# Second score product of the 64-wide heads over 128 partitions instead of 64, with 33 instead of 30 big tiles

## Chip, cores and metric

The kernel runs on one core of a Trainium2 chip. The metric is the device time of one execution in microseconds. The kernel before took 2614.11 us (median of three runs, 2605.13 to 2625.22).

## What is computed

A two-layer encoder trunk over 1024 tokens of width 1024, in float32. Each layer is a mixer of two kinds of attention side by side, then a SwiGLU with 2816 hidden features, each with a scaled residual and a layer norm.

```python
for layer in range(DEPTH):
    if layer % 2 == 0:
        mix = _mixer_ab(x, ...)     # latent attention (8 heads) | sliding-window attention (8 heads, 2 k/v heads)
    else:
        mix = _mixer_cd(x, ...)     # forgetting attention (8 heads) | chunked attention with relative bias (8 heads)
    x = _layer_norm(DEEPNORM_ALPHA * x + mix, ln1_g[layer], ln1_b[layer])
    ffn = _swiglu(x, w_gate, w_up, w_down)
    x = _layer_norm(DEEPNORM_ALPHA * x + ffn, ln2_g[layer], ln2_b[layer])
```

Three of the four kinds have heads of 64 features whose scores are `q . k / 8` plus a bias: the sliding window (`swa`), the forgetting heads (`fox`) and the chunked heads. The latent heads have 96 features and are not touched by the change.

## The kernel before

**Products in two parts.** Float32 numbers are held as a high part of type float32r and the rest, a low part. A product of two such numbers is three matmuls into one PSUM tile (`mm3`, L127): high by high, high by low, low by high. A 64-wide head needs only half of the 128 rows of TensorE for one product, so two of the three are put into one matmul: for the fox and chunked heads, k lies as [high; low] over the 128 partitions and q as [high; high], and L591 in `qk64` contracts over all 128. The third product, q's low part by k's high part, contracts over 64 partitions (L592: rows `r : r + 64` of the tile `ql`, which two heads share, one in the upper and one in the lower half). The sliding-window heads do the same with the sides exchanged: q is [high; low], k is [high; high] (`kk`), L860 contracts over 128, and L861 multiplies q's high part by k's low part (`kl`, two k/v heads in one tile) over 64.

**Attention rows.** `attention_row` is one block of 128 queries of one head; `swa_row` is one block of four heads. A row has stages: `a` (scores on TensorE; L524 on VectorE adds the bias and takes the running maximum; L529 on ScalarE is the exponential), `n` (L533 reciprocal on VectorE, L534 the division on GpSimd), `t` (L551 transposes on TensorE, L106/L107 split into parts), `v` (L562 product with v), `m` (merge and store). A row of over 512 keys has its scores in two pieces, so two PSUM tiles. There are 16 rows of `swa` and, in layer 1, 16 heads of eight rows each. `stream` runs them as a software pipeline: at each step a new row does `a`, the row before it `n`, the one before that `t`, and so on, and between the stages `pump` lets in dense work that the next group needs (projections, L127 into tiles `pd`). The fox heads' bias tile comes from ScalarE or, for the block on the diagonal, from GpSimd (L718, L719).

**Projections of a pair of heads.** `pair_jobs` projects q and k for two heads; `q_evac` writes q's parts from PSUM: L606 high part on ScalarE, L607 a DMA that copies it into the other half, L608 low part on VectorE. GpSimd also makes the low parts of the weights (L117).

**Tiles and order.** The pool `gp` has 30 tiles of 128 x 1024 (`g`) which hold activations, q, k, v, x in both parts, and more. A tile's place is taken when a program instruction first writes it and is given back after its last reader; the Tile scheduler sets the order of each engine's instructions when the program is built, with the pools' free places as one of its conditions. All DMAs are issued from the queue of SyncE.

Of the kernel before, what the change touches and what calls it, by code (L numbers as in the profile page):

```python
# [14 lines left out]
ALU = mybir.AluOpType  # L15
# [5 lines left out]
P = 128  # L21
# [11 lines left out]
CFG = dict(gp=30, wrp=3, whp=5, sp=3, hp=3, bp=2, tp=2, pd=3, ps=2, pt=2, pv=1)  # L33


def fv(ap):
    return ap.bitcast(F32)


class Core:  # L40
# [137 lines left out]
    def ln_pipe(self, y, g, b, xt, done):  # L178
        """Layer norm of one token tile after the other, each one's stages apart; the last ones take the shortest way."""
# [30 lines left out]
    @staticmethod  # L210
    def feat(xt, k, half):
        """Features of tile k for half of the tokens, as a high and a low part."""
        return tuple(x[k // 2][half][:, k % 2, :] for x in xt)
# [6 lines left out]
    def winograd(self, r, b):  # L220
        """The four sums of 2 x 2 blocks that the one side of a product takes; b(i) is a block of the side, r their tiles."""
        for i, (x, z, op) in enumerate(b):
            self.nc.gpsimd.tensor_tensor(r[i], fv(x), fv(r[z] if isinstance(z, int) else z), op=op)

    def sums_x(self, xt):
        """Sums of blocks (feature tiles 0, 1, 4 or 2, 3, 5) x (half of the tokens), as lists of low and high parts by tile."""
# [32 lines left out]
    def cross(self, out, w, x, first, last):  # L259
        """High times low and low times high parts of a block."""  # L260
        for i, (a, b) in enumerate(zip(w, x)):
            self.nc.tensor.matmul(out, a, b, start=first and i == 0, stop=last and i == len(w) - 1)  # L262

    def gate_up(self, wg, wu, xt, xs, more):
        """Gate and up products of one tile for all tokens; over the first feature tiles, the products of high with low
        parts are a Winograd form of the 2 x 2 blocks (gate, up) x (features) x (tokens), with seven instead of eight."""
# [113 lines left out]
def chain(jobs):  # L380
    """Dense jobs (prep, body): each one's weights are fetched while the one before runs."""
    ready = jobs[0][0]()
    for i, (_, body) in enumerate(jobs):
        now, ready = ready, jobs[i + 1][0]() if i + 1 < len(jobs) else None
        yield from body(now)
# [7 lines left out]
class Mixers(Core):  # L393
    def stream(self, groups):
        """Rows of attention in a software pipeline; between their stages, the dense work that the next group needs."""
# [67 lines left out]
    def out_weights(self, wo, kts, j0, j1, tile):  # L463
        """Weights j0 to j1 of the eight that four row tiles of the output projection have."""
# [121 lines left out]
    def qk64(self, qt, ql, kt, r):  # L586
        nc = self.nc

        def f(p, i, c, w):
            q = slice(i * P, i * P + P)  # L590
            nc.tensor.matmul(p, qt[:, q], kt[:, c : c + w], start=True, stop=False)  # L591
            nc.tensor.matmul(p, ql[r : r + HD, q], kt[r : r + HD, c : c + w], start=False, stop=True)  # L592
# [3 lines left out]
    def pair_jobs(self, xt, wqk, i0, out, open_ln=None):  # L596
        """q and k of two 64-wide heads; k is [hi; lo] over the partitions, q is [hi; hi] and its low part apart."""
# [3 lines left out]
        def q_evac(p, o):  # L601
            if "q" not in tiles:
                tiles["q"] = out["q"] = [self.g() for _ in range(3)]
            qa, qb, ql = tiles["q"]
            for t, r in ((qa, 0), (qb, HD)):
# [50 lines left out]
    def mixer_cd(self, xt, wqk, wv, wf, bf, relb, o_scr, c_scr, out_early, open_ln):  # L656
# [18 lines left out]
        def make(n):  # L675
            def rows():
                typ, pair = n // 4, n % 4
                r = []
                for hh in range(2):
# [21 lines left out]
                    r += self.attention_rows(pre, self.qk64(qk[n]["q"][hh], qk[n]["q"][2], qk[n]["k"][hh], hh * HD),  # L701
# [23 lines left out]
    def forget_gate(self, xt, w, bf, c_scr):  # L725
# [17 lines left out]
        # min(z, 0) - log1p(exp(-|z|)), log1p(u) = 2 artanh(u / (2 + u))  # L743
# [33 lines left out]
    def swa_kv(self, xt, wqs, sinks, w):  # L777
# [5 lines left out]
        kk, kl = [self.g() for _ in range(2)], self.g()  # L783
        for half in range(2):
            o = slice(half * 512, half * 512 + 512)
            p = self.fproj(w, xt, half)
            for v in range(2):
# [3 lines left out]
                nc.vector.tensor_tensor(kl[r, o], p[r], fv(kk[v][r, o]), op=ALU.subtract)  # L791
# [50 lines left out]
    def swa_row(self, g, i, qs, bt, pre, o_scr):  # L842
        nc = self.nc
        kk, kl, vs, sk, nsk = self.swa_state
        zr = slice(g * HD, g * HD + HD)
# [7 lines left out]
        def a():  # L853
            sb = st["s"] = self.s().rearrange("p (h k) -> p h k", k=256)
            mx = self.m(4, "mx")
            for hp in range(2):
                p = self.pss().rearrange("p (h k) -> p h k", k=256)
                for z in range(2):
                    h = hp * 2 + z
                    nc.tensor.matmul(p[:, z, 0:kw], qs[h][:, q], kk[g][:, ks], start=True, stop=False)  # L860
                    nc.tensor.matmul(p[:, z, 0:kw], qs[h][zr, q], kl[zr, ks], start=False, stop=True)  # L861
# [375 lines left out]
```

## Time and profile before

| what | value |
|---|---|
| runs, median (lowest to highest) | 2614.11 us (2605.13 to 2625.22) |
| profiled execution, span | 2610.2 us |
| PE busy (matmul) | 2543.0 us, 97% |
| DVE, ACT, POOL busy | 52%, 37%, 52% |
| DMA, mean | 66 GB/s |

The span is read against its own engines: PE is TensorE's matmul row, PEld its weight loads, DVE is VectorE, ACT ScalarE, POOL GpSimd. A matmul's busy time has a modelled end, so it overlaps the next one's; what a matmul costs the queue is the distance to the next. The program runs the sliding window with the projections of the latent heads first (to some 205 us), then the latent heads, the output projection and the SwiGLU of layer 0 (to some 1180 us), then the fox and chunked heads of layer 1 (some 1235 to 1840 us), and then its output projection and SwiGLU.

### The profile page before, as it was taken

How to read it: one execution, taken by the hardware profiler on the slowest of the kernel's cores; microseconds unless marked ns; L12 is line 12 of the kernel's file. 1: busy time of each engine (PE TensorE's matmuls, PEld its weight loads, DVE VectorE, ACT ScalarE, POOL GpSimd, SP SyncE). 2: the span in 40 equal slices, each digit the busy share in tenths (PEclk: the TensorE clock that was granted, in tenths of full speed). 3: DMA queues.
4: the chain of work that ended last, by engine and by line, in shares of the span. 5: the costliest groups of instructions: out<-in, count | busy, mean ns of one | idle time of the engine just before them, and what ended most of it. 6: DMA issues, size and time to landing. Idle time of an engine off the chain costs nothing.

```text
span 2610.2 us, 35589 instructions
## 1 busy us (share of the span) xinstructions
PE 2543.0 (97%) x12376; PEld 2082.6 (80%) x12376; DVE 1360.7 (52%) x3096; ACT 970.9 (37%) x2112; POOL 1350.2 (52%) x1586
## 2 busy tenths in 40 slices
PE   8998999999999999999999999999899999999997
PEld 7976878788888888877778787877778888888886
DVE  3467766734444444447355555456734444444457
ACT  5366766422222222223355655454432222222221
POOL 3332465785555555555345443353765555555565
PEclk9999999999999999999999999999999999999999
DMA  4225241211111111122221111140211111111112
GB/s 149 71 79 166 73 133 53 67 45 53 49 49 49 49 54 56 53 70 97 68 62 50 55 43 50 41 160 26 85 37 49 54 52 49 49 53 49 49 53 97
DMA packets 103923, 172.66 MB, mean 66 GB/s; under 512 B 12728, under 2 KB 38712, under 8 KB 103744
## 3 DMA queue, kind: packets, MB, share of 16 engines
q1 hardware_dynamic: 103744, 170.39, 21.8%
q8 instruction: 98, 1.61, 0.3%
q14 instruction: 81, 0.66, 0.1%
HBM read 143.57 MB, written 22.58 MB: 64 GB/s over the span
## 4 chain that ended last, share of the span: by engine, by line
PE 87%; DVE 4%; POOL 3%; DMA 2%; ACT 2%; issue 1%; SPq 0%; POOLq 0%; DVEq 0%; ACTq 0%
PE pd L127 24%; PE ps L127 18%; PE pd L285 17%; PE pd L262 6%; PE pt L262 6%; PE pv L562 4%; PE pt L551 3%; PE ps L592 2%; PE pv L262 2%; PE ps L591 1%; POOL g L164 1%; DVE g L192 1%; DMA wr<-o_scr 1%; PE ps L861 1%; DVE m L162 1%
## 5 line engine op out<-in xcount | busy, mean ns | idle before, releaser
L117 POOL TENSOR_TENSOR wh<-wr,wh 128x512 fp32r<-128x512 f32 (+2 forms) x363 | 481.8, 1336 | 648.7 <-ACT wh L116 636.3
L127 PE MATMUL pd<-g,wh 128*128 128x512 f32 (+1 forms) x2076 | 540.1, 405 | 19.1 <-ACT g L106 10.1
L285 PE MATMUL pd<-g,wh 128*128 128x512 f32 x1984 | 501.7, 389 | 0.0
L116 ACT CAST wh<-wr 128x512 fp32r<-128x512 f32 (+2 forms) x363 | 222.1, 613 | 745.3 <-PE pd L285 429.1
L127 PEld LDWEIGHTS pd<-g,wh 128*128 128x128 f32 (+1 forms) x2076 | 381.1, 190 | 113.9 <-issue 15.0
L127 PE MATMUL ps<-wh,h 128*128 128x512 f32 x1920 | 462.1, 391 | 1.0 <-DVE g L365 1.0
L285 PEld LDWEIGHTS pd<-g,wh 128*128 128x128 f32 x1984 | 372.4, 188 | 77.3
L127 PEld LDWEIGHTS ps<-wh,h 128*128 128x128 f32 x1920 | 360.6, 188 | 77.7 <-DVE g L365 3.3
L365 DVE TENSOR_TENSOR g<-ps,g 128x512 f32<-128x512 f32 x288 | 197.1, 689 | 321.8 <-PE ps L127 321.8
L534 POOL TENSOR_SCALAR s<-s,m 128x128 f32<-128x128 f32 (+1 forms) x192 | 138.7, 723 | 203.1 <-DVE m L533 183.0
L107 DVE TENSOR_TENSOR h<-pt,h 128x512 fp32r<-128x512 f32 (+3 forms) x318 | 170.3, 544 | 74.1 <-ACT h L106 72.7
L106 ACT CAST h<-pt 128x512 fp32r<-128x512 f32 (+3 forms) x318 | 145.7, 473 | 149.4 <-PE pt L551 138.1
L562 PE MATMUL pv<-h,g 128*128 128x256 f32 x928 | 163.2, 297 | 4.0 <-ACT h L106 2.5
L529 ACT ACTIVATE s<-s,m 128x128 f32<-128x128 f32 (+1 forms) x192 | 144.0, 750 | 58.8 <-DVE m L527 51.6
L127 PE MATMUL pd<-wh,g 128*128 128x256 f32 (+2 forms) x1056 | 159.4, 297 | 0.0
L127 PEld LDWEIGHTS pd<-wh,g 128*128 128x128 f32 x1056 | 141.5, 192 | 7.1 <-issue 5.0
L296 DVE TENSOR_TENSOR t<-pd,t 128x512 f32<-128x512 f32 x160 | 106.9, 686 | 71.5 <-PE pd L262 62.1
L562 PEld LDWEIGHTS pv<-h,g 128*128 128x128 f32 x928 | 128.9, 190 | 17.0 <-ACT h L106 5.1
L551 PE MATMUL pt<-ident,s 128*128 128x128 f32 x816 | 134.4, 276 | 2.8 <-DVE h L107 1.1
L296 DVE TENSOR_TENSOR t<-pt,t 128x512 f32<-128x512 f32 x80 | 55.3, 692 | 152.9 <-PE pt L262 150.8
L551 PEld LDWEIGHTS pt<-ident,s 128*128 128x128 f32 x816 | 96.7, 140 | 20.3 <-issue 6.0
L262 PE MATMUL pt<-g,b 128*128 128x512 f32 x320 | 105.0, 389 | 0.0
(190 smaller groups left out, 3823.5 us busy)
## 6 DMA issues: line engine op xcount, KB each, us to landing
wr<-in_wgu SPq DMA_DIRECT2D x176, 256.0 KB, 2.7
wr<-in_wd SPq DMA_DIRECT2D x88, 256.0 KB, 2.6
o_scr<-t SPq DMA_DIRECT2D x128, 64.0 KB, 2.1
wr<-o_scr SPq DMA_DIRECT2D x32, 256.0 KB, 2.9
wr<-in_cd_f SPq DMA_DIRECT2D x32, 256.0 KB, 2.7
s<-in_xT SPq DMA_DIRECT2D x16, 256.0 KB, 5.2
g<-qr_scr SPq DMA_DIRECT2D x32, 128.0 KB, 3.1
g<-kr_scr SPq DMA_DIRECT2D x16, 256.0 KB, 4.6
```

Source lines behind the costliest of these rows:

```text
L106: self.nc.scalar.copy(hi, src)
L107: self.nc.vector.tensor_tensor(lo, src, fv(hi), op=ALU.subtract)
L116: self.nc.scalar.copy(hl[:, 0, :], raw)
L117: self.nc.gpsimd.tensor_tensor(hl[:, 1, :], raw, fv(hl[:, 0, :]), op=ALU.subtract)
L127: self.nc.tensor.matmul(out, stat[a], mov[c], start=first and i == 0, stop=last and i == 2)
L262: self.nc.tensor.matmul(out, a, b, start=first and i == 0, stop=last and i == len(w) - 1)
L285: nc.tensor.matmul(p, hl[:, a, c], x, start=k + i == 0, stop=extra is None and k == KT - 1 and i == 2)
L296: nc.vector.tensor_tensor(o, x, z, op=ALU.add)
L365: nc.vector.tensor_tensor(y[tt][:, o], p, y[tt][:, o], op=ALU.add)
L529: nc.scalar.activation(sb[:, 0:w], sb[:, 0:w], AF.Exp, bias=neg, scale=scale, accum_out=sm)
L551: nc.tensor.transpose(tp[:, (kb - b0) * P : (kb - b0) * P + P], sb[:, (kb - k0) * P : (kb - k0) * P + P], self.ident)
L562: nc.tensor.matmul(pv, vt(kb), pair[kb // 4][:, l, kb % 4, :], start=c == 0, stop=c == 2 * (last + 1 - first) - 1)
```

## The change

The second score product is taken over all 128 partitions. For the fox and chunked heads each head gets a low tile of its own whose other half is zero (two tiles of a pair where one was, so four tiles for q and not three); GpSimd writes the zeros once for a pair of heads. The same is done for `kl` in the sliding window. TensorE's instructions have the same number and the same columns. The pool `gp` gets 33 tiles, and the place comes from a smaller reserve in SBUF for DMA descriptors (1 KB a partition).

```diff
-CFG = dict(gp=30, wrp=3, whp=5, sp=3, hp=3, bp=2, tp=2, pd=3, ps=2, pt=2, pv=1)
+CFG = dict(gp=33, wrp=3, whp=5, sp=3, hp=3, bp=2, tp=2, pd=3, ps=2, pt=2, pv=1)
...
-    def qk64(self, qt, ql, kt, r):
+    def qk64(self, qt, ql, kt):
...
-            nc.tensor.matmul(p, ql[r : r + HD, q], kt[r : r + HD, c : c + w], start=False, stop=True)
+            nc.tensor.matmul(p, ql[:, q], kt[:, c : c + w], start=False, stop=True)
...
         def q_evac(p, o):
             if "q" not in tiles:
-                tiles["q"] = out["q"] = [self.g() for _ in range(3)]
-            qa, qb, ql = tiles["q"]
-            for t, r in ((qa, 0), (qb, HD)):
+                tiles["q"] = out["q"] = [self.g() for _ in range(4)]
+                for ql, r in zip(tiles["q"][2:], (0, HD)):
+                    nc.gpsimd.memset(fv(ql[HD - r : P - r, :]), 0.0)
+            for t, ql, r in zip(tiles["q"][:2], tiles["q"][2:], (0, HD)):
                 nc.scalar.mul(t[r : r + HD, o], p[r : r + HD], 0.125)
                 nc.sync.dma_start(fv(t[HD - r : P - r, o]), fv(t[r : r + HD, o]))
                 nc.vector.scalar_tensor_tensor(ql[r : r + HD, o], p[r : r + HD], 0.125, fv(t[r : r + HD, o]),
...
-        kk, kl = [self.g() for _ in range(2)], self.g()
+        kk, kl = [self.g() for _ in range(2)], [self.g() for _ in range(2)]
+        for v in range(2):
+            nc.gpsimd.memset(fv(kl[v][HD - v * HD : P - v * HD, :]), 0.0)
...
-                nc.vector.tensor_tensor(kl[r, o], p[r], fv(kk[v][r, o]), op=ALU.subtract)
+                nc.vector.tensor_tensor(kl[v][r, o], p[r], fv(kk[v][r, o]), op=ALU.subtract)
...
-                    nc.tensor.matmul(p[:, z, 0:kw], qs[h][zr, q], kl[zr, ks], start=False, stop=True)
+                    nc.tensor.matmul(p[:, z, 0:kw], qs[h][:, q], kl[g][:, ks], start=False, stop=True)
...
-    nc = _bacc.Bacc("TRN2", target_bir_lowering=False, num_devices=1)
+    nc = _bacc.Bacc("TRN2", target_bir_lowering=False, num_devices=1, dynamic_dma_scratch_size=1024)
```

The scheduler's order changes with it, at two stretches of the program: in the latent heads (some 290 to 430 us of the trace) and in the fox and chunked heads (some 1290 to 1660 us). On PE the counts and kinds of instructions are the same. On PE, at the third to fifth row of the first fox head, the score products (L591, L592 into the tiles `ps`) stand among the dense products of the next pair (L127 into `pd`). Before:

```order
L591 MATMUL ps_12222<-g_11665,g_11631 128x384
L592 MATMUL ps_12222<-g_11665,g_11633 128x384
L127 MATMUL pd_12358<-g_6246,wh_12177 128x512
L127 MATMUL pd_12358<-g_6254,wh_12177 128x512
L127 MATMUL pd_12196<-g_6247,wh_12182 128x512 x2
L127 MATMUL pd_12196<-g_6255,wh_12182 128x512
L127 MATMUL pd_12196<-g_6247,wh_12182 128x512
L591 MATMUL ps_12252<-g_11665,g_11631 128x512
L592 MATMUL ps_12252<-g_11665,g_11633 128x512
```

The same place on PE after:

```order
L591 MATMUL ps_12228<-g_11671,g_11634 128x384
L592 MATMUL ps_12228<-g_11671,g_11636 128x384
L591 MATMUL ps_12258<-g_11671,g_11634 128x512
L592 MATMUL ps_12258<-g_11671,g_11636 128x512
L127 MATMUL pd_12367<-g_6251,wh_12188 128x512 x2
```

The pairs of score products are the same; here two rows' pairs now stand next to each other, and the dense products follow them.

On DVE, at the q projection of the third pair of heads, L608 (L610 after) takes q's low part out of the PSUM tiles of the two halves of the tokens. Before:

```order
L608 SCALAR_TENSOR_TENSOR g_13063<-pd_12911,g_13061 64x512
L524 ISA s_12547,m_12551<-ps_12548,t_12552 128x256
...
L608 SCALAR_TENSOR_TENSOR g_13063<-pd_13070,g_13061 64x512
L527 TENSOR_SCALAR m_12595<-m_12588 128x1
...
L608 SCALAR_TENSOR_TENSOR g_13063<-pd_12911,g_13062 64x512
L527 TENSOR_SCALAR m_12837<-m_12830 128x1
L527 TENSOR_SCALAR m_12884<-m_12877 128x1
L608 SCALAR_TENSOR_TENSOR g_13063<-pd_13070,g_13062 64x512
```

After, with the two low tiles `g_13072` and `g_13073`:

```order
L610 SCALAR_TENSOR_TENSOR g_13072<-pd_12920,g_13070 64x512
L610 SCALAR_TENSOR_TENSOR g_13073<-pd_12920,g_13071 64x512
L524 ISA s_12556,m_12560<-ps_12557,t_12561 128x256
...
L610 SCALAR_TENSOR_TENSOR g_13072<-pd_13082,g_13070 64x512
L524 ISA s_12593,m_12597<-ps_12594,t_12598 128x384
...
L610 SCALAR_TENSOR_TENSOR g_13073<-pd_13082,g_13071 64x512
```

Before, the second head's part of the first PSUM tile stands 52 rows behind the first head's (row 1612 against 1560), since its `g` tile has no place yet; after, it stands right behind it, and both PSUM tiles are free within 16 rows.

On POOL, at the same pair, the new zeros (L606) stand among the bias work of the diagonal blocks (L720 and L721, which were L718 and L719) and a weight's low part (L117). Before:

```order
L534 TENSOR_SCALAR s_12379<-s_12379,m_12461 128x896
L117 TENSOR_TENSOR wh_13175<-wr_13174,wh_13175 128x512
L718 TENSOR_SCALAR t_12589<-b_12377,cq 128x384
L718 TENSOR_SCALAR t_12636<-b_12377,cq 128x512
L719 AFFINE_SELECT t_12589<-t_12589 128x128
```

After:

```order
L534 TENSOR_SCALAR s_12388<-s_12388,m_12470 128x896
L721 AFFINE_SELECT t_12561<-t_12561 128x128
L117 TENSOR_TENSOR wh_13187<-wr_13186,wh_13187 128x512
L606 MEMSET g_13073 64x1024
L720 TENSOR_SCALAR t_12598<-b_12386,cq 128x384
L720 TENSOR_SCALAR t_12645<-b_12386,cq 128x512
L721 AFFINE_SELECT t_12598<-t_12598 128x128
```

The zeros of the second low tile are new in the row; this one waits for a reader on PE of what its place held before, and the bias tiles of the diagonal blocks and the divisions L534 are queued behind it.

## Rows read from the trace of the kernel before

**Rows 1.** The page: the span, then part 1, busy time by engine.
```profile
span 2610.2 us, 35589 instructions
PE 2543.0 (97%) x12376; PEld 2082.6 (80%) x12376; DVE 1360.7 (52%) x3096; ACT 970.9 (37%) x2112; POOL 1350.2 (52%) x1586
```

**Rows 2.** Busy us (instructions) of PE, PEld, DVE, ACT, POOL by stretch; PEclk, DMA.
```profile
55.00:205.00 150.00, 148.80 (x789) 124.15 (x788) 82.03 (x342) 80.56 (x261) 57.40 (x117) 0.98 0.27 81
205.00:300.00 95.00, 82.74 (x460) 69.75 (x460) 71.64 (x203) 63.66 (x163) 30.90 (x50) 0.95 0.47 131
...
1235.00:1840.00 605.00, 598.44 (x3289) 471.81 (x3290) 320.38 (x1074) 315.00 (x749) 254.70 (x420) 0.98 0.22 64
```

**Rows 3.** Lines 592 and 861: count, ns min/median/max, starts, rows*columns and columns streamed.
```profile
L592 PE MATMUL ps<-g,g x192: 322/438/686, 1235.6 to 1829.2; 64*128 64x384 f32 x80, 64*128 64x256 f32 x56, 64*128 64x512 f32 x40, 64*128 64x128 f32 x16
...
L861 PE MATMUL ps<-g,g x64: 322/381/579, 55.7 to 201.9; 64*128 64x256 f32 x56, 64*128 64x128 f32 x8
```

**Rows 4.** The chain of waits in order, fox heads: start us, us on the chain, what.
```profile
1406.82 0.96 PE pv L562 x8
...
1414.27 0.17 PE ps L591
1414.44 0.37 PE ps L592
1414.81 0.43 PE pd L127
...
1417.07 2.76 PE pd L127 x12
1419.82 0.23 PE ps L591
1420.05 0.42 PE ps L592
1420.47 0.90 PE pd L127 x3
1421.37 0.44 PE pt L551 x4
```

**Rows 5.** The same view in the sliding window.
```profile
196.43 0.32 PE ps L860
196.75 0.31 PE ps L861
197.06 0.60 PE pt L888 x4
```

**Rows 6.** Timeline of weight loads, fox heads: start us, us, what, [idle before, until].
```profile
1406.55 1.02 PEld L562 LDWEIGHTS pv<-h,g 128*128 128x128 f32 x8
...
1408.93 0.18 PEld L592 LDWEIGHTS ps<-g,g 64*128 64x128 f32 x1 [0.17 <-issue]
```

**Rows 7.** What PE waited for, 1240 to 1840 us: total us, times, longest; first and last.
```profile
PE ps L591 <- DVE m L524: 3.2, 10, 0.8
...
PE pd L127 <- ACT s L116: 0.2, 1, 0.2
```

**Rows 8.** Groups by line, 1240 to 1840 us: count, busy us, mean ns, idle before.
```profile
L529 ACT ACTIVATE s<-s,m 128x640 f32<-128x640 f32 (+7 forms) x128 | 94.2, 736 | 42.6 <-DVE m L527 37.7 <-DVE m L533 4.2
L534 POOL TENSOR_SCALAR s<-s,m 128x640 f32<-128x640 f32 (+7 forms) x128 | 90.7, 710 | 131.5 <-DVE m L533 127.4 <-DVE m L527 1.3 <-PE ps L592 1.2
...
L562 PEld LDWEIGHTS pv<-h,g 128*128 128x128 f32 x596 | 83.0, 191 | 10.6 <-issue 3.3 <-ACT h L106 1.8 <-DVE m L527 0.9
...
L524 DVE CUSTOM_DVE_ANT_0 s<-ps,t 128x384 f32<-128x384 f32 (+2 forms) x64 | 35.6, 557 | 34.2 <-PE ps L592 15.0 <-PE pt L551 13.8 <-POOL t L719 3.8
```

**Rows 9.** Groups by line and form on POOL, whole span: the nearest memsets.
```profile
L546 POOL MEMSET h<- 128x256 f32 x112 | 34.6, 313 | 82.7 <-PE pv L562 77.3 <-DVE m L533 2.8 <-PE pv L895 2.3
...
L766 POOL MEMSET s<- 8x1024 f32 x1 | 0.9, 943 | 0.0
```

**Rows 10.** The page, part 3: the DMA queue that carries the kernel's transfers.
```profile
q1 hardware_dynamic: 103744, 170.39, 21.8%
```

More of the change, by code (lines that the diff above doesn't have):

```diff
@@ L700, in rows @@
                         self.o_dst(o_scr, kt, hh * HD, q0, 256), o.rearrange("p (t c) -> p t c", c=P))
-                    r += self.attention_rows(pre, self.qk64(qk[n]["q"][hh], qk[n]["q"][2], qk[n]["k"][hh], hh * HD),
+                    r += self.attention_rows(pre, self.qk64(qk[n]["q"][hh], qk[n]["q"][2 + hh], qk[n]["k"][hh]),
                                              bias, vt, 1.0, lo, dst)
@@ L844, in swa_row @@
         kk, kl, vs, sk, nsk = self.swa_state
-        zr = slice(g * HD, g * HD + HD)
         g4 = slice(g * 4, g * 4 + 4)
```

## The prediction

> **What bounds the kernel now.** I read the page's busy times first: TensorE's matmuls fill 2543 of 2610 us, the other engines about half or less [rows 1]. Since a matmul's end is modelled, that alone does not say that TensorE is the limit in the stages that the change touches, so I took the busy times by stretch: in the sliding window (55 to 205 us) PE has 148.8 of 150 us, in the fox and chunked heads (1235 to 1840 us) 598.4 of 605 us, while the busiest other engine, VectorE, has 82 of 150 and 320 of 605 [rows 2]. What PE waits for in 1240 to 1840 us is seven rows that come to 5.8 us, of which the longest single wait is 0.8 us [rows 7]. So both stages run at the pace at which PE takes its instructions, and what a matmul costs is its distance from the one before. That is what the chain of waits gives, since there each piece ends where the next starts.
>
> **What a 64-row matmul costs.** There are 192 of them on L592 and 64 on L861, 256 in all [rows 3]. First the clean pace of 128-row matmuls: eight of 256 columns take 0.96 us, 0.12 each; twelve of 512 columns take 2.76 us, 0.23 each; L591 with 384 columns takes 0.17; four transposes take 0.44, 0.11 each [rows 4]. Now the visits. At 1414.44 us L592 with the same 384 columns takes 0.37 (0.20 more than L591), and the 128-row matmul behind it, of 512 columns, takes 0.43 (0.20 more). At 1420.05 us L592 with 512 columns takes 0.42 (0.19 more), and the three matmuls behind it 0.90 for a clean 0.69 (0.21 more) [rows 4]. Both visits cost 0.40 us. In the sliding window the 64-row L861 (256 columns) takes 0.31 and the L860 behind it 0.32, both 0.12 when clean: 0.39. Where transposes follow a visit it is 0.19 and 0.60 - 0.44 = 0.16, so 0.35 [rows 5]. The surcharge thus hardly depends on the columns, and half of it lies on the 64-row matmul and half on its successor.
>
> Why it is there shows in the weight loads: eight loads before L562 take 1.02 us together although one lasts 0.19 [rows 8], so they lie under each other's matmuls; the load of L592 starts only after 0.17 us in which the load path stood still for nothing that the trace names [rows 6]. Going from 128 rows to 64 and back, a load is not hidden. I can't see the reason inside the array, and don't need it: after the change every score matmul has 128 rows, as L591 and L860 have, and these run at the clean pace wherever no 64-row one is next to them.
>
> **The page that speaks against it.** The Trainium skill, "TensorE: Matmul & The Clock Gate", Part 3, The mechanism, says that a weight load overlaps with matmuls in flight only when its row group differs. By it, two 128-row matmuls, which share all row groups, could not hide a load, and a third product over 128 rows would gain nothing: the sum would be 0 and the time 2614. The trace does not bear it out, since loads of 0.19 us run at 0.12 us per matmul in those rows.
>
> **The sum, part by part.**
> - The product: 256 visits x 0.39 us = 100 us less on PE, 75 in the fox and chunked heads and 25 in the sliding window. Bounds: 0.35 gives 90, 0.40 gives 102. Columns and the number of instructions stay, so nothing is added on PE.
> - The zeros: 16 memsets in layer 1 and two in the sliding window, each 64 x 1024, a form the trace does not have. 8 x 1024 takes 0.94 us, 128 x 256 takes 0.31, so four times that is 1.25 [rows 9]. I take 0.95, as the partitions seem to cost nothing, which makes 17 us of GpSimd in all (22 at the upper bound). GpSimd is busy 255 of 605 us there [rows 2], and a pair of heads needs its zeros only when its own scores start, a projection later. On the path: 0. Without that cover it would be the 17 to 22 us. What is queued behind a memset is the bias of diagonal blocks, the divisions L534 and the weights' low parts, as the order on POOL shows; that is a rival below.
> - The low part on VectorE has the same count and shape, written to two tiles. In the order on DVE the two heads' low parts now leave their PSUM tile together; that can only free `pd` sooner. Today PE shows no large wait for it [rows 7], so I put it at 0.
> - 33 places: two are eaten by the fourth q tile (two pairs are alive at once), one by `kl`, so layer 1 has one place more than it needs and the latent heads two. The upper bound of what this may give is PE's idle time where stages meet, 12 us in 205 to 300 us [rows 2]; the lower bound is a less lucky order at that place, which I let cost as much again. I take 0.
> - The descriptor reserve: all but a few of the transfers run on the hardware queue [rows 10], and none is issued by GpSimd. 0.
>
> **What is given back.** With PE 75 us faster over 605, the other engines' shares rise: VectorE from 0.53 to 320 / 530 = 0.60. None becomes the bound on average. By row: 128 rows in 605 us are 4.7 us each, later 4.1. Scores and transposes of a row are two steps apart in the program, so 9.5 us now and 8.3 after; between them lie one or two maxima (0.56 each), the exponential (0.74) and the division (0.71) [rows 8], some 2.6 us and small column operations. That is ample on average, but the scheduler's order lets some rows come closer, and those now meet data that isn't there. The two ends are nothing given back and half of it (50 us). Because today's waits are 1% of the stretch, I take a value near the lower end: one visit in five loses its gain, 20 us.
>
> Sum: 2610.2 - 100 + 20 = 2530 for the profiled execution. The median of the runs lies 4 us above that execution's span (2614.1 against 2610.2), so **2534 us**.
>
> **Rivals.**
> 1. All of it arrives, and the new places take some waits at the seams: 2610 - 100 - 6 + 4 = 2508. For it: short waits now [rows 7]. Against it: a pipeline that is a tenth faster must meet some late data. 0.15.
> 2. Half is given back, since rows at the end of a head wait for maxima and exponentials, and L591 for its PSUM tile, which is the longest wait today [rows 7]: 2610 - 50 + 4 = 2564. Against it: VectorE at 0.60. 0.18.
> 3. No gain. Either the page's rule holds for these tiles, or the surcharge comes from adding a second product into the same PSUM tile rather than from 64 rows: 2614. Against the second: the twelve dense matmuls at 0.23 also add into one tile [rows 4]. 0.07.
> 4. Slower. A memset of a `g` tile whose former reader is still ahead on PE holds GpSimd's queue, and the divisions behind it come late for the transposes. A pair's memsets hold up PE only beyond the cover of 8.3 - 2.6 = 5.7 us. There are nine places (eight pairs and the window), so the gain of 100 is used up when each holds GpSimd for 5.7 + 11 = 17 us, four rows long; at 20 us each it is 9 x 14.3 = 129 lost: 2610 - 100 + 129 + 4 = 2643. Against it: the scheduler puts a memset where its reader is due. 0.05.
>
> **Chances.** The forecast (2518 to 2550) has 0.55, the rivals the rest. About 1%, 26 us, is what a measurement of this kernel can tell from no change. Faster than 2588 is the forecast, rival 1 and rival 2: 0.88; within 1% is rival 3: 0.07; slower 0.05. The range reaches down to rival 1 with the upper bound of a visit (102) and a little of the seams, 2505, and up past rival 2 to where most of its half lies, 2572.
>
> **What would show it.** In the changed kernel L592 and the line of L861 show 128 rows, their pieces on the chain are 0.17 and 0.23 for 384 and 512 columns and 0.12 for 256, and the piece behind them is clean; the stalls of the load path before L592 are gone. The stretch of layer 1 shrinks by 60 to 75 us and the sliding window by 20 to 25, all other stages stay within a few us. PE's waits for POOL, ACT and DVE in the fox and chunked heads rise from 6 to some 20 us. GpSimd has 18 memsets of about 0.95 us. The prediction is wrong if the 128-row form of L592 still takes 0.37, if PE's waits in layer 1 rise over 40 us, or if the seam of 205 to 300 us changes by more than 12 us.

## The result and the profile after

The changed kernel takes **2533.3 us** (median of four runs, 2531.6 to 2534.4) beside 2609.9 us for the kernel before, measured with it: a ratio of 0.9705, 95% interval 0.9673 to 0.9738. The profiled execution has a span of 2532.6 us, 77.6 less than the 2610.2 of before. The prediction was 2534, with a range of 2505 to 2572.

The page of the changed kernel, the span and part 1:

```profile
span 2532.6 us, 35601 instructions
PE 2452.3 (97%) x12376; PEld 2067.3 (82%) x12376; DVE 1358.9 (54%) x3096; ACT 970.8 (38%) x2112; POOL 1365.9 (54%) x1604
```

Beside [rows 1], PE's busy time has fallen by 91 us and that of the weight loads by 15, and GpSimd has 18 instructions and 16 us more; VectorE and ScalarE are as they were. The next fence is the table by stretch, in the columns of [rows 2]; the stretches are those of the same work, the sliding window, the seam behind it, and layer 1's heads.

```profile
55.00:188.00 133.00, 126.82 (x789) 114.74 (x787) 80.07 (x338) 80.26 (x261) 56.69 (x116) 1.00 0.30 89
188.00:283.00 95.00, 83.31 (x470) 71.36 (x471) 73.24 (x210) 64.61 (x171) 31.44 (x51) 0.95 0.47 134
...
1213.00:1763.00 550.00, 532.71 (x3283) 465.55 (x3284) 318.95 (x1073) 314.86 (x746) 266.57 (x434) 0.98 0.24 71
```

The window is some 17 us shorter and layer 1's heads some 55 to 56; all the other stages together account for the 4 to 5 us that are left of 77.6. The seam is as idle as it was, 11.7 us against 12.3. PE is no longer full in the two stages: 126.8 of 133 and 532.7 of 550, where it had 148.8 of 150 and 598.4 of 605. VectorE's share in layer 1's heads is now 0.58.

The line of the second product, as in [rows 3], with its weight loads above it; first the weight loads of before and what stood before them, then the changed kernel, and last the window's second product in the changed kernel:

```profile
L592 PEld LDWEIGHTS ps<-g,g x192: 182/183/285, 1235.6 to 1829.2; 64*128 64x128 f32 x192
  issue: 34.4, 143
```

```profile
L592 PEld LDWEIGHTS ps<-g,g x192: 187/188/295, 1213.4 to 1750.7; 128*128 128x128 f32 x192
L592 PE MATMUL ps<-g,g x192: 272/337/481, 1213.4 to 1750.8; 128*128 128x384 f32 x80, 128*128 128x256 f32 x56, 128*128 128x512 f32 x40, 128*128 128x128 f32 x16
its engine sat idle before it (us, times) until:
who waited for it (us, times):
```

```profile
L864 PE MATMUL ps<-g,g x64: 274/280/363, 55.7 to 185.0; 128*128 128x256 f32 x56, 128*128 128x128 f32 x8
```

Counts and columns are those of before, the rows are 128, the median matmul falls from 438 to 337 ns, and below "sat idle before it" nothing stands any more, where the load path had stood for 34.4 us at 143 places. From the first to the last L592 it is 537.4 us, where it was 593.6; from the first to the last product of the window it is 129.3, where it was 146.2.

### The profile page after: what moved, and what is told of

Read it like the earlier page. It is cut to its first block, busy times and chain, and to the rows that moved or that the text cites. A ratio compares the mean times of both kernels' runs of the same rounds, so it can differ in the third digit from the quotient of the medians.

```text
span 2532.6 us, 35601 instructions
## 1 busy us (share of the span) xinstructions
PE 2452.3 (97%) x12376; PEld 2067.3 (82%) x12376; DVE 1358.9 (54%) x3096; ACT 970.8 (38%) x2112; POOL 1365.9 (54%) x1604
## 4 chain that ended last, share of the span: by engine, by line
PE 85%; DVE 5%; POOL 3%; DMA 3%; ACT 2%; issue 2%; SPq 0%; POOLq 0%; DVEq 0%; ACTq 0%
PE pd L127 24%; PE ps L127 19%; PE pd L285 17%; PE pd L262 6%; PE pt L262 6%; PE pv L562 4%; PE pt L551 3%; PE pv L262 2%; POOL g L164 1%; PE ps L591 1%; PE ps L592 1%; DVE g L192 1%; DVE m L162 1%; DMA wr<-o_scr 1%; ACT g L163 1%
## 5 line engine op out<-in xcount | busy, mean ns | idle before, releaser
L117 POOL TENSOR_TENSOR wh<-wr,wh 128x512 fp32r<-128x512 f32 (+2 forms) x363 | 482.3, 1337 | 666.9 <-ACT wh L116 637.1
L127 PE MATMUL pd<-g,wh 128*128 128x512 f32 (+1 forms) x2076 | 530.9, 401 | 19.2 <-ACT g L106 10.1
L285 PE MATMUL pd<-g,wh 128*128 128x512 f32 x1984 | 501.8, 389 | 0.0
L127 PEld LDWEIGHTS pd<-g,wh 128*128 128x128 f32 (+1 forms) x2076 | 382.7, 189 | 103.8 <-ACT g L106 11.0
L127 PE MATMUL ps<-wh,h 128*128 128x512 f32 x1920 | 460.9, 390 | 1.0 <-DVE g L365 1.0
L285 PEld LDWEIGHTS pd<-g,wh 128*128 128x128 f32 x1984 | 372.4, 188 | 77.3
L127 PEld LDWEIGHTS ps<-wh,h 128*128 128x128 f32 x1920 | 359.5, 188 | 77.4 <-DVE g L365 3.2
L534 POOL TENSOR_SCALAR s<-s,m 128x128 f32<-128x128 f32 (+1 forms) x192 | 138.1, 720 | 174.0 <-DVE m L533 147.8
L107 DVE TENSOR_TENSOR h<-pt,h 128x512 fp32r<-128x512 f32 (+3 forms) x318 | 170.0, 543 | 47.3 <-ACT h L106 45.5
L106 ACT CAST h<-pt 128x512 fp32r<-128x512 f32 (+3 forms) x318 | 145.5, 472 | 119.2 <-PE pt L551 111.4
L562 PE MATMUL pv<-h,g 128*128 128x256 f32 x928 | 160.8, 295 | 5.2 <-ACT h L106 4.3
L127 PE MATMUL pd<-wh,g 128*128 128x256 f32 (+2 forms) x1056 | 158.9, 296 | 0.8 <-DVE t L967 0.6
L127 PEld LDWEIGHTS pd<-wh,g 128*128 128x128 f32 x1056 | 145.2, 194 | 3.5 <-PE pt L939 0.8
L562 PEld LDWEIGHTS pv<-h,g 128*128 128x128 f32 x928 | 129.4, 190 | 13.7 <-ACT h L106 6.6
L551 PE MATMUL pt<-ident,s 128*128 128x128 f32 x816 | 133.4, 274 | 6.5 <-DVE h L107 3.8
L551 PEld LDWEIGHTS pt<-ident,s 128*128 128x128 f32 x816 | 98.5, 141 | 20.3 <-issue 6.1
```

The source lines that it names most:

```text
L106: self.nc.scalar.copy(hi, src)
L107: self.nc.vector.tensor_tensor(lo, src, fv(hi), op=ALU.subtract)
L117: self.nc.gpsimd.tensor_tensor(hl[:, 1, :], raw, fv(hl[:, 0, :]), op=ALU.subtract)
L127: self.nc.tensor.matmul(out, stat[a], mov[c], start=first and i == 0, stop=last and i == 2)
L285: nc.tensor.matmul(p, hl[:, a, c], x, start=k + i == 0, stop=extra is None and k == KT - 1 and i == 2)
L551: nc.tensor.transpose(tp[:, (kb - b0) * P : (kb - b0) * P + P], sb[:, (kb - k0) * P : (kb - k0) * P + P], self.ident)
```

## The experiments

All medians are in microseconds. Since the kernel before scatters between 2605 and 2626 from run to run, each kernel is set against the runs of the kernel before that were taken beside it. The ratio and its interval come from those runs and are not the quotient of the two medians (for e3 that would be 0.9966). A stretch inside a kernel is read from one profiled execution of each, so differences of one or two microseconds between such stretches carry no weight.

| kernel | median | before, beside it | ratio (95%) |
|---|---|---|---|
| changed kernel | 2533.3 | 2609.9 | 0.9705 (0.9673 to 0.9738) |
| e1, 33 tiles and small reserve alone | 2609.0 | 2620.5 | 0.9970 (0.9951 to 0.9989) |
| e3, changed, products over 64 rows | 2611.7 | 2620.5 | 0.9991 (0.9971 to 1.001) |
| e4, changed, window's product over 64 rows | 2551.3 | 2620.5 | 0.9766 (0.9723 to 0.9808) |
| e5, before, 41 visits fewer | 2605.4 | 2620.5 | 0.9943 (0.9920 to 0.9967) |
| e6, changed, zeros four times | 2543.7 | 2607.4 | 0.9748 (0.9722 to 0.9773) |
| e7, changed, no division | 2538.0 | 2607.4 | 0.9729 (0.9700 to 0.9758) |
| e7, before, no division | 2600.8 | 2607.4 | 0.9977 (0.9961 to 0.9992) |
| e8, changed, 2 dense and 3 score tiles of PSUM | 2555.8 | 2607.4 | 0.9791 (0.9764 to 0.9818) |
| e2, changed, 30 tiles and old reserve | 2539.2 | 2608.8 | 0.9734 (0.9719 to 0.9750) |
| e10, changed, lasting zeros | 2529.8 | 2608.8 | 0.9701 (0.9687 to 0.9716) |
| e11, changed, score and v tiles pooled | 2535.0 | 2608.8 | 0.9715 (0.9698 to 0.9731) |
| e12, changed, dense and score tiles pooled | 2526.0 | 2608.8 | 0.9687 (0.9673 to 0.9702) |

### The product alone, in the same order (e3)

```diff
...
-            nc.tensor.matmul(p, ql[:, q], kt[:, c : c + w], start=False, stop=True)
+            nc.tensor.matmul(p, ql[r : r + HD, q], kt[r : r + HD, c : c + w], start=False, stop=True)
...
-                    nc.tensor.matmul(p[:, z, 0:kw], qs[h][:, q], kl[g][:, ks], start=False, stop=True)
+                    nc.tensor.matmul(p[:, z, 0:kw], qs[h][g * HD : g * HD + HD, q], kl[g][g * HD : g * HD + HD, ks], start=False, stop=True)
```

> The changed kernel, with its zeros, tiles and reserve, but both second products again over the 64 rows that aren't zero. Theory: 256 visits at 0.39 us come back less the 20 us that were given back, so 2533 + 80 = 2613 us, and a few us more for zeros that now buy nothing. Rival (order and tiles): it stays under 2570 us.

It took 2611.7. This is the sharpest comparison of the study, since e3 has the instructions of the changed kernel in the same order on every engine; only the rows of 256 matmuls differ. Its span is 2612.4 us against 2532.6, so the product alone is worth **79.8 us** by the profiled executions and 78.4 by the medians. Of the 79.8, some 5.5 us lie at matmuls where TensorE's granted clock was at the lower of its two levels, 1.2 GHz, in only one of the two executions (over the span the clock is 0.986 in e3 and 0.990 in the changed kernel); whether that comes from the change was not tested. The first fence is e3's line, the second its chain of waits at two score pieces of one row late in the chunked heads; the third is the chain of the changed kernel at the very same instructions.

```profile
L592 PEld LDWEIGHTS ps<-g,g x192: 182/183/285, 1233.6 to 1831.8; 64*128 64x128 f32 x192
L592 PE MATMUL ps<-g,g x192: 322/435/792, 1233.6 to 1831.8; 64*128 64x384 f32 x80, 64*128 64x256 f32 x56, 64*128 64x512 f32 x40, 64*128 64x128 f32 x16
its engine sat idle before it (us, times) until:
  issue: 34.2, 141
```

```profile
1731.99 0.17 PE ps L591
1732.16 0.37 PE ps L592
1732.53 0.32 PE ps L591
1732.85 0.31 PE ps L592
1733.16 0.89 PE pd L127 x3
```

```profile
1664.05 0.18 PE ps L591
1664.23 0.17 PE ps L592
1664.40 0.12 PE ps L591
1664.52 0.12 PE ps L592
1664.64 2.52 PE pd L127 x11
```

Two visits: 0.37 - 0.17, 0.32 - 0.12, 0.31 - 0.12, and 0.89 - 3 x 0.23 make 0.79 us, 0.395 each. With 128 rows nothing of it is left. The stalls of the load path in front of L592, 34.2 us at 141 places, are gone too. Over all 256 visits, the distances of e3's matmuls beyond the clean pace of their like come to some 96 us, 72 in layer 1's heads and 24 in the window: 0.39 each where a dense product, another score product or the product with v follows, 0.34 where transposes follow, and 0.29 to 0.34 for most of the 24 visits with only 128 columns.

From e3 to the changed kernel, layer 1's heads (first to last L592) go from 598.2 to 537.4, 61 of the 75 us that the prediction booked for 192 visits and of the 72 that they measure.

### The tiles alone (e1) and the product without them (e2)

```diff
-CFG = dict(gp=30, wrp=3, whp=5, sp=3, hp=3, bp=2, tp=2, pd=3, ps=2, pt=2, pv=1)
+CFG = dict(gp=33, wrp=3, whp=5, sp=3, hp=3, bp=2, tp=2, pd=3, ps=2, pt=2, pv=1)
...
-    nc = _bacc.Bacc("TRN2", target_bir_lowering=False, num_devices=1)
+    nc = _bacc.Bacc("TRN2", target_bir_lowering=False, num_devices=1, dynamic_dma_scratch_size=1024)
```

e1 is this in the kernel before; e2 is the changed kernel with these two lines as they were.

> The kernel before with 33 big tiles and the 1 KB descriptor reserve, products as they were. Theory (the 64-row visits carry the gain): within 6 us of the kernel before, some 2610 us, and the visits on the chain keep their 0.37 us for 384 columns. Rival (the three places and the order they allow carry it): 2540 to 2580 us.

> The changed product and its zeros with the 30 big tiles and the descriptor reserve of before. Theory (product -80 us by the same-order comparison, zeros +3, tiles about 0): 2533 to 2540 us, since layer 1 then has one tile less than it had and the second head's projection waits for its place. Rival (the places are needed for the gain): over 2550 us.

e1 took 2609.0, and its line has the 64 rows and the durations of before:

```profile
L592 PE MATMUL ps<-g,g x192: 322/437/792, 1230.9 to 1828.2; 64*128 64x384 f32 x80, 64*128 64x256 f32 x56, 64*128 64x512 f32 x40, 64*128 64x128 f32 x16
```

The profiled spans are 2609.2 and 2610.2, while the interval of the ratio lies just below 1 (0.1 to 0.5% of gain, 3 to 13 us by its ends, against a kernel whose runs scatter by 20). So places and reserve alone do little: the rival that they carry the gain falls. e2 took 2539.2, 5.9 more than the changed kernel by the medians and 3.3 by the spans (2535.9 against 2532.6). With the product changed, the places and the reserve together are thus worth 3 to 6 us; the prediction had them at 0. The expected reason, one place too few in layer 1, is not where it lies: from its first to its last L592, e2 takes 535.6 us (1218.2 to 1753.8), no more than the 537.4 of the changed kernel, and it is already 4.8 us behind at the first. With or without them the product brings its gain.

### The window alone (e4)

The edit is the second one of e3 alone.

> The changed kernel with only the sliding window's second product back over 64 rows (64 visits). Theory with the traces' stage lengths: the window's stretch was 146.2 us from its first to its last L861 before and 129.3 after, so 17 us come back: 2550 us. If all 64 visits at 0.39 us come back in full: 2558 us. If the sliding window is bound by something else, as its transposes' waits would have it: within 5 us of 2533 us.

It took 2551.3, and the window's products have 64 rows again while those of layer 1 have 128:

```profile
L864 PEld LDWEIGHTS ps<-g,g x64: 182/183/183, 56.6 to 201.2; 64*128 64x128 f32 x64
```

By the medians 18 us come back, by the spans 14.2 (2546.8 against 2532.6), and not the 25 of 64 visits; from the first to the last of these products it is 144.6 us against 129.3. So the window gave back a larger share of its gain (a quarter or more) than layer 1's heads (14 of 75). Against e3, where the 64 visits measure 24 us, the window is 16.5 us shorter in the changed kernel.

### Is it the switch or the 64-row matmul (e5)

In the kernel before, the two products of every second score piece change places, which brings two 64-row matmuls next to each other at 41 places. (The sum into PSUM is the same.) The edit in `qk64` is shown; the window's products are turned in the same way for the second head of each pair. The two neighbours lie over the same half of the 128 rows.

```diff
-            nc.tensor.matmul(p, qt[:, q], kt[:, c : c + w], start=True, stop=False)
-            nc.tensor.matmul(p, ql[r : r + HD, q], kt[r : r + HD, c : c + w], start=False, stop=True)
+            turn = i in seen
+            seen[i] = True
+            if turn:
+                nc.tensor.matmul(p, ql[r : r + HD, q], kt[r : r + HD, c : c + w], start=True, stop=False)
+            nc.tensor.matmul(p, qt[:, q], kt[:, c : c + w], start=not turn, stop=turn)
+            if not turn:
+                nc.tensor.matmul(p, ql[r : r + HD, q], kt[r : r + HD, c : c + w], start=False, stop=True)
...
```

> The kernel before with the two products of every second score piece in turned order, so that 64-row matmuls stand next to each other at 41 places (32 in the sliding window) and there are 215 visits to 64 rows and not 256, with the same 256 matmuls of 64 rows. If the surcharge belongs to the switch between 128 and 64 rows: 41 x 0.39 = 16 us less, 2594 us, and a second 64-row matmul at 0.12 us for 256 columns on the chain. If it belongs to every 64-row matmul: 2610 us, and the second one costs what the first does.

The chain of waits of e5 in the window; L871 and L868 are the 64-row products, L869 the 128-row one, all of 256 columns:

```profile
102.15 0.79 PE pd L127 x6
102.94 0.31 PE ps L871
103.25 0.12 PE ps L868
103.37 0.43 PE ps L869 x2
103.80 0.31 PE ps L871
104.11 0.12 PE ps L868
104.23 0.32 PE ps L869
```

The first 64-row matmul takes 0.31, the second one 0.12, which is the clean pace, and the 128-row product behind the pair carries the other 0.20 (0.43 for two). So the surcharge is one of the switch to 64 rows and back, and not one of the 64-row matmul: two of them in a row pay it once. Two over different halves next to each other were not run. The time bears it out, a ratio of 0.9943, or 15 us less than the kernel before beside it, where 41 x 0.39 = 16 were expected. The median of 2605 lies over the 2594 that the expectation named: of e5's ten runs four lie at 2595.8 to 2596.8 and six at 2604.6 to 2609.8, and those of the kernel before beside it fall into two groups as well, eight at 2605.6 to 2611.2 and seventeen from 2615.0 on. Group against group e5 is 11 to 15 us faster.

### The zeros (e6, e10)

e6 repeats each memset four times; e10 keeps four low tiles through layer 1, so that the zeros are written four times there and not sixteen.

```diff
-                    nc.gpsimd.memset(fv(ql[HD - r : P - r, :]), 0.0)
+                    for _ in range(4):
+                        nc.gpsimd.memset(fv(ql[HD - r : P - r, :]), 0.0)
```

```diff
-                tiles["q"] = out["q"] = [self.g() for _ in range(4)]
-                for ql, r in zip(tiles["q"][2:], (0, HD)):
-                    nc.gpsimd.memset(fv(ql[HD - r : P - r, :]), 0.0)
+                n = i0 // 2
+                if n < 2:
+                    self.lasting[n] = [self.g() for _ in range(2)]
+                    for ql, r in zip(self.lasting[n], (0, HD)):
+                        nc.gpsimd.memset(fv(ql[HD - r : P - r, :]), 0.0)
+                tiles["q"] = out["q"] = [self.g() for _ in range(2)] + self.lasting[n % 2]
```

> The changed kernel with each memset of zeros four times, so 54 more memsets at 0.95 us, 51 us more work for GpSimd. Theory (GpSimd has the room): within 5 us of the changed kernel, 2533 to 2538 us. Rival (the zeros hold up the divisions or the bias of the diagonal blocks, and are part of what was given back): a third of the 51 us shows or more, over 2550 us.

> The changed kernel with four low tiles that two pairs use in turn through all of layer 1, so that their zeros are written four times and not sixteen. By the price that the fourfold zeros showed (7 to 10 us for 51 us of GpSimd), 12 memsets or 11 us less of GpSimd bring 2 us: 2531 us. If the zeros stood in nobody's way: 2533 us. If tiles that never change place cost the order its room: 2536 to 2545 us.

In the changed kernel, the groups of the new memsets on GpSimd (count, busy us, mean ns, idle before them):

```profile
L606 POOL MEMSET g<- 64x1024 f32 x16 | 15.2, 948 | 2.0 <-PE pv L562 0.7 <-PE ps L591 0.6
L787 POOL MEMSET g<- 64x1024 f32 x2 | 1.9, 948 | 0.1
```

Then what PE waited for in layer 1's heads in e6, the first row:

```profile
PE ps L591 <- DVE m L524: 10.6, 20, 1.4
```

A memset takes 0.95 us, as estimated, and GpSimd stood only 2 us for the tiles' former readers. But more zeros are not free: e6 has 54 memsets or 51 us more of GpSimd and takes 10 us more by the medians (7 by the spans, 2539.5 against 2532.6), more than the 5 that theory allowed and less than the rival's third. Its runs (2541.3 to 2546.2) lie clear of those of the changed kernel. The scores' wait for the maximum rises to 10.6 us (it is 6.5 in the changed kernel, below). If the price is proportional, the 17 us of zeros cost 2 to 3.5 us. Two other comparisons have the same sign, but don't settle it. e3 takes 2611.7 and e1, without zeros and split low tiles, 2609.0; yet e3 is 2.7 us behind already at the first L592 of layer 1, when two of the 18 memsets have run. e10, with 12 memsets less, took 2529.8, 3.5 us less than the changed kernel; but its granted clock in layer 1's heads was 1.00 where the changed kernel had 0.98, which may be as much of a reason.

### Where the rest was given back (e7, e8, e11, e12)

e7 leaves the division of the probabilities out but for 8 columns, in the changed kernel and in the one before. e8 gives PSUM two dense and three score tiles. e11 puts the score tiles and the tile of the products with v into one pool of three, e12 the dense and the score tiles into one of five.

```diff
-            nc.gpsimd.tensor_scalar(sb[:, 0:w], sb[:, 0:w], rc, 1.0, op0=ALU.mult, op1=ALU.mult)
+            nc.gpsimd.tensor_scalar(sb[:, 0:8], sb[:, 0:8], rc, 1.0, op0=ALU.mult, op1=ALU.mult)
```

```diff
-CFG = dict(gp=33, wrp=3, whp=5, sp=3, hp=3, bp=2, tp=2, pd=3, ps=2, pt=2, pv=1)
+CFG = dict(gp=33, wrp=3, whp=5, sp=3, hp=3, bp=2, tp=2, pd=2, ps=3, pt=2, pv=1)
```

```diff
...
-        self.pv = pool("pv", CFG["pv"], space=PSUM)
...
-        return self.pv.tile([P, 512], F32, tag="v", name=self.nm("pv"))
+        return self.ps.tile([P, 512], F32, tag="s", name=self.nm("pv"))
```

```diff
...
-        self.ps = pool("ps", CFG["ps"], space=PSUM)
...
-        return self.ps.tile([P, 512], F32, tag="s", name=self.nm("ps"))
+        return self.pd.tile([P, 512], F32, tag="d", name=self.nm("ps"))
```

> The changed kernel without the division of the probabilities in the latent, fox and chunked rows (the division is done for 8 columns only, the rest is left out), so that a row's way from its scores to its transposes is some 0.7 us shorter and GpSimd has 110 us less work. Theory (what was given back in the fox and chunked heads, 75 - 59 = 16 us, are PE's waits for rows whose maxima, exponentials and divisions come late): 5 to 12 us less than 2533, and twice what the same cut brings the kernel before. Rival (it was lost elsewhere, at seams): the same few us in both kernels.

> The same cut in the kernel before (division for 8 columns only, the rest left out): the control for the run above. Theory: 0 to 5 us less than the kernel before, since its rows have more cover. Rival: as much as in the changed kernel.

> The changed kernel with two PSUM tiles for dense products and three for scores (three and two so far). PE's largest named wait in layer 1's heads is L591 for the maximum L524 that still reads its PSUM tile (6.5 us of 17). If that is what was given back: 5 to 8 us less, 2526 us. If two tiles for dense products are too few, the projections wait for their evictions: 2540 to 2600 us.

> The changed kernel with the PSUM tile of the products with v put into one pool with the two of the scores (three in common). PE's waits for a free score tile are the largest of those that remain in layer 1's heads (L591 for L524, 6.5 us named). Theory (these waits hold back part of the gain): 4 to 8 us less, 2525 to 2529 us. Rival (the order, not the number of tiles, makes the wait, or the products with v then wait for scores): 2533 us or more, as with two dense and three score tiles (2556 us).

> The changed kernel with the three dense and the two score PSUM tiles in one pool of five. Theory: a score finds a free tile more often, and dense products seldom need three: 3 to 8 us less, 2525 to 2530 us. Rival: dense work runs ahead and takes the tiles that scores need: 2540 us or more.

What PE waited for in layer 1's heads, first the changed kernel (1213 to 1763 us), then e3 at the same work (1232 to 1842 us), the rows that differ most:

```profile
PE ps L591 <- DVE m L524: 6.5, 11, 1.8
PE pt L551 <- DVE h L107: 3.0, 5, 1.3
PE pv L562 <- ACT h L106: 1.9, 3, 1.0
```

```profile
PE ps L591 <- DVE m L524: 5.8, 11, 0.9
PE pt L551 <- DVE h L107: 1.3, 2, 0.8
...
PE pv L562 <- ACT h L106: 0.6, 1, 0.6
```

All named waits of that view come to 17.0 us in the changed kernel (eleven rows) and to 11.1 in e3 (nine rows): 5.9 us more, of the 14 that are missing from 75. In the window, the changed kernel shows the following, the first of which e3 has not at all (of the second it has 0.4):

```profile
PE pt L891 <- POOL s L883: 2.6, 4, 1.1
PE pv L898 <- DVE t L579: 1.3, 2, 0.8
```

There the division on GpSimd (L883) comes late for the transposes, as the prediction thought of a faster pipeline, but the named waits are again shorter than what is missing.

The distances of the matmuls, set side by side in the same order, show where most of the rest is. In the changed kernel the places of the former visits hold 18 us beyond the clean pace, 15 in layer 1's heads and 3 in the window, and the rest of the window 6 us more than in e3. In layer 1's heads, the 86 second products that a dense product follows wait 0.6 us in all (0.4 in e3); the 89 that are followed by a row's transposes (L551) or its product with v (L562) wait 12.5 us (4.3 in e3), at 17 places. There the next matmul needs the split parts that ScalarE (L106) and VectorE (L107) write (L562), or a PSUM tile that they empty (L551), and most of these waits end with one of the two. The named waits show less of it than there is, since a matmul's modelled end reaches over the start of the next (a matmul of 256 columns lasts 0.28 us at a distance of 0.12). No run changed the splits, so that they are the cause is indicated and not tested.

The division does not account for it either, as far as e7 goes. Without it GpSimd has 51 us less to do in that stretch (215.94 against 266.57), and the changed kernel takes 2538.0, not less than 2533, while the kernel before gains 7 us. Theory and rival both fall here: the kernel before gains more and not half as much. But the total hides a shorter layer 1, because the cut also changes the order. The dense line L285 stands in the SwiGLU of either layer; its first and last starts there, in the changed kernel and then in e7, are:

```profile
L285 PE MATMUL pd<-g,wh x992: 389/389/389, 545.5 to 1147.1; 128*128 128x512 f32 x199
L285 PE MATMUL pd<-g,wh x992: 389/389/389, 1871.3 to 2472.9; 128*128 128x512 f32 x199
```

```profile
L285 PE MATMUL pd<-g,wh x992: 388/389/389, 551.4 to 1153.2; 128*128 128x512 f32 x199
L285 PE MATMUL pd<-g,wh x992: 389/389/389, 1870.8 to 2472.3; 128*128 128x512 f32 x199
```

From layer 0's SwiGLU to layer 1's it is 724.2 us in the changed kernel and 717.6 in e7, 6.7 less, while 6 us are lost ahead of layer 0's. In the kernel before the same stretch goes from 783.0 to 771.4, 11.6 less. So leaving out the division gains something in layer 1, more in the slower kernel than in the faster one; that a faster pipeline waits more for it is not borne out. These are single executions, and the same stretch differs by 2.4 us between e4 and the changed kernel, which have the same instructions there.

The score tiles are not it alone either. e8 took 2555.8; these are PE's largest waits over its whole span:

```profile
PE pd L127 <- ACT g L106: 12.3, 6, 6.1
PE pd L991 <- DVE g L997: 6.2, 3, 5.3
PE ps L591 <- DVE m L524: 5.6, 11, 1.6
```

The first is hardly more than in the changed kernel, where the same row has 10.1 us; the second is new there, and the third, the one that a third score tile should shorten, has barely fallen from 6.5. Some 22 us are lost by the end of the window and the seam behind it, where the dense products run.

In e11 the named wait for a score tile in layer 1's heads falls to 2.3 us (L591 stands on line 590 there), and the median stays at 2535.0:

```profile
PE ps L590 <- DVE m L523: 2.3, 5, 0.6
```

e12 took **2526.0**, 7.3 us less than the changed kernel and the fastest of all that were run, with its wait for a score tile at 4.6 us. That a pool of five helps was expected; that it helps through this wait does not show, since its gain is there before layer 1's heads begin. This is the line that is L285 above (one line higher in e12), in layer 0:

```profile
L284 PE MATMUL pd<-g,wh x992: 389/389/389, 557.6 to 1139.0; 128*128 128x512 f32 x199
```

Its last start is 8.1 us ahead of the changed kernel's 1147.1, and the end of the span is 8.3 ahead (2524.3 against 2532.6). Whether the pool would bring as much in the kernel before was not run. So it is a better kernel, and no proof of where the missing 14 and 8 us went.

## Why the prediction was right

**What bounds it.** Right. PE filled both stages, and taking 0.39 us off 256 places shortened both.

**The price of a visit.** Right in kind, and a little high. Its two halves, on the 64-row matmul and on its successor, are both gone in the changed kernel, 0.395 us per visit at the same two places of e3; and e5 shows that it is paid per change of rows and back. Over all 256 visits it comes to 96 us and not 100, as those before transposes and those of 128 columns cost less. The place of the stall was the weight load, as [rows 6] had it: 34.2 us of standing load path in e3, none after.

**The page against it.** In the changed kernel the loads of 128-row matmuls behind one another are hidden, 0.17 and 0.12 us per score matmul with loads of 188 ns, and in e3 those that go from 128 rows to 64 or back are the ones that stand out. The Trainium skill, "TensorE: Matmul & The Clock Gate", Part 3, The mechanism, says that a weight load overlaps with matmuls in flight only when its row group differs. The runs do not agree with that sentence, by which the change would have brought nothing. The Trainium skill says in the same section that a load into the background weight buffer is pulled ahead of matmuls in flight as well. By that, nothing in the section stood against the change; the prediction weighed the one sentence alone.

**The sum.** 100 us off, 20 given back, net 80: the same-order comparison has 79.8. By stage the forecast was 60 to 75 in layer 1's heads and 20 to 25 in the window, and both came out lower against the kernel before: 56.2 (593.6 to 537.4) and 16.9 (146.2 to 129.3), with 4 to 5 us from other stages, which the sum had at 0. Against e3 it is 61 and 16.5. The window lost more than its share, which the sum had not split.

**The zeros.** The duration was right (0.95). "On the path: 0" may have been 2 to 3.5 us too low by the price that e6 shows; e10 and e3 against e1 don't settle it.

**The tiles.** Taken at 0. Alone they are small, as taken; beside the changed product they and the reserve are worth 3 to 6 us (e2), which the sum left out. The seam of 205 to 300 us did not move.

**What is given back.** The size was about right, the reason only in part. The named waits in layer 1's heads were to rise from 6 to some 20 us; they are 17.0, against 8.1 in the same stretch of the kernel before and 11.1 in e3. The late data are mostly not those that were named (maxima, exponentials, division): most of what is missing stands where a row's transposes or its product with v follow the score product, behind the splits on ScalarE and VectorE, which the prediction's 2.6 us for a row left out, and e7 does not bear out that the division holds back more in the faster kernel.

**Luck.** That 2534 met 2533.3 within a microsecond is partly luck. The visits were worth some 96 us and not 100; beyond the clean pace stand 18 us at their places and 6 more in the window; zeros cost 0 to 3.5 and places gave 3 to 6, both booked at 0; and of the difference from e3 some 5.5 us go with the granted clock. These have opposite signs. The mechanism and the size of its main term were not luck.

**Rivals.** All of it arriving (2508): no. Half (2564): no. The rival of no gain falls with e3 against the changed kernel. The slower one, a memset that holds GpSimd: GpSimd stood 2.1 us in all before the memsets, where this rival needed 17 us at each of nine places.

## What to carry to other kernels

Among 128-row matmuls, a matmul over 64 rows was dearer here than the same one padded with zeros to 128: look at the chain of waits for a matmul whose piece, and whose successor's piece, is longer than that of its like with all rows, and at "issue" in front of its weight load. Where padding is not to be had, put 64-row matmuls over the same half of the rows next to each other, since the switch was paid once for two of them (e5). When such a saving is booked, ask which waits the slower engine had covered: here about a fifth did not arrive, most of it where the next matmul needs fresh data. And compare in the same instruction order, as the same program with its operands sliced gives it.

## What the runs showed of the hardware that was not expected

The price of the switch hardly depends on columns or on the number of 64-row matmuls: 0.39 us for one with 256, 384 or 512 columns (0.34 before transposes, 0.29 to 0.34 for most with 128 columns, in e3), and about the same for two over the same half of the rows (e5).

A memset of 64 x 1024 on GpSimd takes 948 ns, and one of 8 x 1024 took 943 [rows 9]: the number of partitions hardly mattered.

In the profiled executions of e5 and e11 the same VectorE addition, which takes 0.69 us as a rule and 1.3 to 1.6 at this place in the others, took 20.48 and 19.81 us, and PE stood 10.7 and 10.3 us behind it (timeline of DVE in e5 and in e11, then a row of PE's waits in e5):

```profile
1919.19 20.48 DVE L107 TENSOR_TENSOR h<-t,h 128x512 fp32r<-128x512 f32 x1 [0.69 <-ACT h L106]
```

```profile
1862.40 19.81 DVE L106 TENSOR_TENSOR h<-t,h 128x512 fp32r<-128x512 f32 x1 [0.69 <-ACT h L105]
```

```profile
PE ps L127 <- DVE g L363: 10.7, 1, 10.7
```

In both it ends 0.55 us after the end of an unbroken run of GpSimd's additions (to 1939.12 in e5, to 1881.66 in e11). That this run held it up is argued from the times alone; it was not tested. Such a pause sits inside the span of one execution (2602.9 in e5, 2545.9 in e11, 11 us above e11's median), so spans with it should not be compared with spans without.
